# Engine programs without a block, loads released by matmul groups, larger evictions and an aligned TensorE loop in a batched matmul

## The chip, the cores and the metric

The kernel runs on one core of a Trainium2 chip. The metric is the device time of one execution in microseconds (us), as the median of several executions. A profiled execution also gives a span, from its first to its last instruction, which is about 2 us shorter than the time.

## The reference

```python
batch, m, k, n = 16, 512, 768, 1024      # x: [16, 768, 512], y: [16, 768, 1024], fp32
def reference(x, y):
    return np.einsum('bkm,bkn->bmn', x, y).astype(np.float32)
```

Each of the 16 batches loads 4.7 MB (x and y), multiplies, and stores 2.1 MB.

## The kernel before

SP (the SyncE engine) issues all transfers on one queue, VectorE casts x and y to bf16, TensorE multiplies in a loop of two batches per turn, and ScalarE copies PSUM to the output buffers. Input buffers are double, so the load of batch b reuses the buffers of batch b-2. Batches count from 0: the third load is that of batch 2, and where the prediction writes "load 3" it means batch 3. A release is the wait that lets SP issue a transfer, a landing is the semaphore count with which one of the 16 DMA engines reports the end of its part, and a hole is a time in which DMA engines have nothing to move. In the views PE is TensorE (PEld its weight loads), DVE VectorE, ACT ScalarE; a q marks the engine's sequencer, which waits and issues. `batch, i, first` of the TensorE program and the tensors are cut here.

```python
    @block.sync
    def _(sync):
        def store(b):
            sync.wait_ge(outs, b + 1)
            sync.dma_start(o_v[b], ob[b % NO][:]).then_inc(so[b % NO], 16)
        for b in range(B):
            i = b % 2
            if b >= 2:
                sync.wait_ge(cast, b - 1)            # both casts of batch b-2 are done
            sync.dma_start(xs[i][:], x_v[b]).then_inc(sx[i], 16)
            sync.dma_start(ys[i][:], y_v[b]).then_inc(sy[i], 16)
            if b >= LAG:                             # LAG = 4: the first store follows the fifth load
                store(b - LAG)
        # ... the last stores, the waits for all stores
    @block.vector
    def _(vector):
        for b in range(B):
            # ... wait for TensorE and for x; cast x, wait for y, cast y in two halves
            vector.drain().then_inc(cast, 1)
    @block.tensor
    def _(tensor):
        with tensor.Fori(0, B // 2):
            batch(tensor, 0, False)                  # 48 matmuls in 4 groups of 12
            batch(tensor, 1, False)
    @block.scalar
    def _(scalar):
        # ... one copy of 128x1024 for each group, then
            scalar.drain().then_inc(outs, 1)
```

## Time and profile before

| | before |
|---|---|
| time, median (first 3 runs) | 262.83 us |
| span | 261.2 us |
| DMA queue, share of 16 engines' span | 98.1% |
| moved | 109.05 MB |
| TensorE busy | 188.0 us |
| VectorE busy | 83.0 us |
| ScalarE busy | 66.1 us |

For the comparisons below, this is the view by stretches of time of the kernel before. The columns are the stretch, its length, five engines' busy time with instruction counts, TensorE's granted clock, DMA share and GB/s. DMA share is the second last.

```profile
24.00:28.00 4.00, 4.00 (x20) 2.09 (x19) 2.01 (x2) 1.42 (x2) 0.00 (x0) 1.00 0.97 415
...
34.00:36.00 2.00, 2.00 (x11) 1.02 (x9) 0.00 (x0) 0.64 (x1) 0.00 (x0) 1.00 0.85 363
36.00:40.00 4.00, 4.00 (x20) 2.13 (x19) 3.01 (x2) 1.39 (x2) 0.00 (x0) 1.00 1.05 440
...
48.00:52.00 4.00, 3.62 (x17) 1.51 (x15) 2.82 (x2) 2.03 (x2) 0.00 (x0) 1.00 1.03 436
52.00:56.00 4.00, 3.30 (x17) 1.74 (x17) 2.37 (x2) 1.01 (x1) 0.00 (x0) 1.00 1.10 449
```

The share lies between 0.85 and 1.10. It can pass 1, because a packet's whole time is counted in the stretch where it starts; a pause shows as a share clearly below that of the same stretch here.

### The profile page before, as it was taken

How to read it: one execution, taken by the hardware profiler on the slowest of the kernel's cores; microseconds unless marked ns; L12 is line 12 of the kernel's file. 1: busy time of each engine (PE TensorE's matmuls, PEld its weight loads, DVE VectorE, ACT ScalarE, POOL GpSimd, SP SyncE). 2: the span in 40 equal slices, each digit the busy share in tenths (PEclk: the TensorE clock that was granted, in tenths of full speed). 3: DMA queues.
4: the chain of work that ended last, by engine and by line, in shares of the span. 5: the costliest groups of instructions: out<-in, count | busy, mean ns of one | idle time of the engine just before them, and what ended most of it. 6: DMA issues, size and time to landing. Idle time of an engine off the chain costs nothing. (4 is left out here: it accounts for less than half of the span.)

```text
span 261.2 us, 1938 instructions
## 1 busy us (share of the span) xinstructions
PE 188.0 (72%) x768; PEld 87.1 (33%) x768; DVE 83.0 (32%) x48; ACT 66.1 (25%) x65; POOL 0.2 (0%) x4
## 2 busy tenths in 40 slices
PE   0039999998948949398595997939678394896920
PEld 0014555443513515144152342514334142342500
DVE  0261734435223252322524214252132523225000
ACT  1003343433331314114032140412314033131410
POOL 0000000000000000000000000000000000000000
PEclk9999999999986999979798697997999899797995
DMA  7999999999999999999999999999999999999993
GB/s 265 431 425 427 438 411 453 425 386 418 446 420 439 420 430 446 415 441 420 439 437 412 447 423 440 415 432 442 423 434 420 435 433 423 440 433 421 434 421 141
DMA packets 6915, 109.09 MB, mean 418 GB/s; under 512 B 768, under 2 KB 768, under 8 KB 768
## 3 DMA queue, kind: packets, MB, share of 16 engines
q1 hardware_dynamic: 6912, 109.05, 98.1%
q8 instruction: 1, 0.02, 0.0%
q14 instruction: 2, 0.02, 0.0%
HBM read 75.50 MB, written 33.55 MB: 417 GB/s over the span
## 5 line engine op out<-in xcount | busy, mean ns | idle before, releaser
L105 PE MATMUL ps<-yb,xb 128*128 128x512 bf16 x768 | 188.0, 406 | 61.6 <-PEq L100 55.9
L105 PEld LDWEIGHTS ps<-yb,xb 128*128 128x128 bf16 x768 | 87.1, 116 | 162.1 <-issue 96.7
L125 ACT COPY ob<-ps 128x1024 f32<-128x1024 f32 x64 | 64.9, 1013 | 183.6 <-PE ps L105 183.6
L93 DVE CAST yb<-ys 128x3072 bf16<-128x3072 f32 x32 | 54.9, 1757 | 88.4 <-DMA ys<-in_y_dram 88.4
L89 DVE CAST xb<-xs 128x3072 bf16<-128x3072 f32 x16 | 28.2, 1760 | 67.5 <-DMA xs<-in_x_dram 66.8
L125 ACT ACT_TABLE_LOAD x1 | 1.3, 1283 | 1.0 <-SPq L44 1.0
L142 POOL MEMSET const-uint8-127<- 128x1 uint8 x1 | 0.1, 102 | 0.0
L142 POOL MEMSET const-bfloat16-1.0<- 128x1 bf16 x1 | 0.1, 101 | 0.0
L142 POOL MEMSET const-float32-0.0<- 128x1 f32 x1 | 0.1, 98 | 0.2 <-issue 0.2
L142 POOL MEMSET const-float32-1.0<- 128x1 f32 x1 | 0.1, 98 | 0.0
## 6 DMA issues: line engine op xcount, KB each, us to landing
ys<-in_y_dram SPq DMA_DIRECT2D x16, 3072.0 KB, 27.7
out_dram<-ob SPq DMA_DIRECT2D x16, 2048.0 KB, 32.1
xs<-in_x_dram SPq DMA_DIRECT2D x16, 1536.0 KB, 20.8
```

The source lines that it names most:

```text
L89: nc.vector.tensor_copy(xb[i][:], xs[i][:]).then_inc(ready, 1)
L93: nc.vector.tensor_copy(yb[i][:, ks], ys[i][:, ks]).then_inc(ready, 1)
L105: mm = nc.tensor.matmul(ps[mo][:, nt], x_w[:, kt, mo], yb[i][:, kt, nt * NF:(nt + 1) * NF], start=(kt == 0), stop=(kt == KT - 1))
L125: nc.scalar.copy(ob[b % NO][:, mo].rearrange("p (t f) -> p t f", f=NF), ps[mo][:]).then_inc(room, 1)
L142: nc = _bacc.Bacc("TRN2", target_bir_lowering=False, num_devices=1)
```

## The change

The intent is fewer instructions. The block goes, and with it branches and a barrier; VectorE's 16 drains go; ScalarE makes 32 copies of 128x2048 instead of 64 of 128x1024; and the TensorE loop is put at the start of an instruction fetch block. With the drains, the semaphore `cast` is gone as well, so SP now releases loads and most stores by TensorE's group counter. Cut to its core:

```diff
-    ps = [ec(nc.psum_tensor(f"ps{i}", [P, NT, NF], FP32)) for i in range(MT)]
+    HB = MT // 2
+    ps = [ec(nc.psum_tensor(f"ps{i}", [P, HB, NT, NF], FP32)) for i in range(2)]
-    block = ec(nc.Block())
     # stores
-            sync.wait_ge(outs, b + 1)
+        if b < B - 2:
+            nc.sync.wait_ge(groups, 2 * (b + 2))
+        else:
+            nc.sync.wait_ge(outs, b - (B - 3))
     # loads
-                sync.wait_ge(cast, b - 1)
+            nc.sync.wait_ge(groups, 2 * (b - 2) + 1)     # TensorE's first half of batch b-2
     # VectorE
-            vector.drain().then_inc(cast, 1)
     # TensorE: two groups of 24 matmuls a batch
-        with tensor.Fori(0, B // 2):
+    with nc.Fori(0, B // 2, engines=OrderedEngineSet([pe]), head_slot={pe: 0}):
     # ScalarE: one copy of 128x2048 a group; a drain only in batch B - 2
     # ... cut
```

More of the change, by code (lines that the diff above doesn't have):

```diff
@@ L10 @@
 from concourse._compat import with_exitstack
+from concourse.ordered_engine_set import OrderedEngineSet
 @with_exitstack
@@ L41 @@
     KH = KT // 2
-    GP = NT * NF
     ctx.enter_context(tc.tile_critical())
@@ L54 @@
     so = [ec(nc.semaphore(f"so{i}")) for i in range(NO)]
-    cast = ec(nc.semaphore("cast"))
     ready = ec(nc.semaphore("ready"))
@@ L59 @@
     outs = ec(nc.semaphore("outs"))
-    block = ec(nc.Block())
-    @block.sync
-    def _(sync):
-        def store(b):
-            sync.wait_ge(outs, b + 1)
-            sync.dma_start(o_v[b], ob[b % NO][:]).then_inc(so[b % NO], 16)
-        for b in range(B):
-            i = b % 2
-            if b >= 2:
-                sync.wait_ge(cast, b - 1)
-            sync.dma_start(xs[i][:], x_v[b]).then_inc(sx[i], 16)
-            sync.dma_start(ys[i][:], y_v[b]).then_inc(sy[i], 16)
-            if b >= LAG:
-                store(b - LAG)
-        for b in range(B - LAG, B):
-            store(b)
-        for i in range(NO):
-            sync.wait_ge(so[i], 16 * len(range(i, B, NO)))
@@ L81, in _ @@
-    @block.vector
-    def _(vector):
-        for b in range(B):
-            i = b % 2
-            n = 16 * (b // 2 + 1)
-            if b >= 2:
-                vector.wait_ge(groups, MT * (b - 1))
-            vector.wait_ge(sx[i], n)
-            nc.vector.tensor_copy(xb[i][:], xs[i][:]).then_inc(ready, 1)
-            vector.wait_ge(sy[i], n)
-            for h in range(2):
-                ks = slice(h * KH, (h + 1) * KH)
-                nc.vector.tensor_copy(yb[i][:, ks], ys[i][:, ks]).then_inc(ready, 1)
-            vector.drain().then_inc(cast, 1)
@@ L96, in batch @@
-    def batch(tensor, i, first):
-        x_w = xb[i][:].rearrange("p k (j mo) -> p k mo j", mo=MT)
-        tensor.wait_ge(ready, 2).then_inc(ready, -2)
-        for mo in range(MT):
-            tensor.wait_ge(room, 1).then_inc(room, -1)
-            for nt in range(NT):
-                for kt in range(KT):
-                    if mo == 0 and nt == 0 and kt == KH:
-                        tensor.wait_ge(ready, 1).then_inc(ready, -1)
-                    mm = nc.tensor.matmul(
-                        ps[mo][:, nt], x_w[:, kt, mo],
-                        yb[i][:, kt, nt * NF:(nt + 1) * NF],
-                        start=(kt == 0), stop=(kt == KT - 1))
-            mm.then_inc(groups, 1)
@@ L111, in _, with store @@
-    @block.tensor
-    def _(tensor):
-        with tensor.Fori(0, B // 2):
-            batch(tensor, 0, False)
-            batch(tensor, 1, False)
-    @block.scalar
-    def _(scalar):
-        nc.scalar.nop().then_inc(room, MT)
-        for b in range(B):
-            for mo in range(MT):
-                if mo == 0 and b >= NO:
-                    scalar.wait_ge(so[b % NO], 16 * (b // NO))
-                scalar.wait_ge(groups, MT * b + mo + 1)
-                nc.scalar.copy(ob[b % NO][:, mo].rearrange("p (t f) -> p t f", f=NF),
-                               ps[mo][:]).then_inc(room, 1)
-            scalar.drain().then_inc(outs, 1)
+    def store(b):
+        if b < B - 2:
+            nc.sync.wait_ge(groups, 2 * (b + 2))
+        else:
+            nc.sync.wait_ge(outs, b - (B - 3))
+        nc.sync.dma_start(o_v[b], ob[b % NO][:]).then_inc(so[b % NO], 16)
@@ new lines @@
+    for b in range(B):
+        i = b % 2
+        if b >= 2:
+            nc.sync.wait_ge(groups, 2 * (b - 2) + 1)
+        nc.sync.dma_start(xs[i][:], x_v[b]).then_inc(sx[i], 16)
+        nc.sync.dma_start(ys[i][:], y_v[b]).then_inc(sy[i], 16)
+        if b >= LAG:
+            store(b - LAG)
+    for b in range(B - LAG, B):
+        store(b)
+    for b in range(B):
+        i = b % 2
+        n = 16 * (b // 2 + 1)
+        if b >= 2:
+            nc.vector.wait_ge(groups, 2 * (b - 1))
+        nc.vector.wait_ge(sx[i], n)
+        nc.vector.tensor_copy(xb[i][:], xs[i][:]).then_inc(ready, 1)
+        nc.vector.wait_ge(sy[i], n)
+        for h in range(2):
+            ks = slice(h * KH, (h + 1) * KH)
+            nc.vector.tensor_copy(yb[i][:, ks], ys[i][:, ks]).then_inc(ready, 1)
@@ new lines, in batch @@
+    def batch(i):
+        x_w = xb[i][:].rearrange("p k (j mo) -> p k mo j", mo=MT)
+        nc.tensor.wait_ge(ready, 2).then_inc(ready, -2)
+        for g in range(2):
+            nc.tensor.wait_ge(room, 1).then_inc(room, -1)
+            for m in range(HB):
+                for nt in range(NT):
+                    for kt in range(KT):
+                        if g == 0 and m == 0 and nt == 0 and kt == KH:
+                            nc.tensor.wait_ge(ready, 1).then_inc(ready, -1)
+                        mm = nc.tensor.matmul(
+                            ps[g][:, m, nt], x_w[:, kt, g * HB + m],
+                            yb[i][:, kt, nt * NF:(nt + 1) * NF],
+                            start=(kt == 0), stop=(kt == KT - 1))
+            mm.then_inc(groups, 1)
@@ new lines @@
+    pe = nc.tensor.engine
+    with nc.Fori(0, B // 2, engines=OrderedEngineSet([pe]), head_slot={pe: 0}):
+        batch(0)
+        batch(1)
+    nc.scalar.nop().then_inc(room, 2)
+    for b in range(B):
+        if b >= NO:
+            nc.scalar.wait_ge(so[b % NO], 16 * (b // NO))
+        for g in range(2):
+            nc.scalar.wait_ge(groups, 2 * b + g + 1)
+            cp = nc.scalar.copy(ob[b % NO][:, g * HB:(g + 1) * HB].rearrange("p m (t f) -> p m t f", f=NF),
+                                ps[g][:])
+            if b < B - 1:
+                cp.then_inc(room, 1)
+        if b == B - 2:
+            nc.scalar.drain().then_inc(outs, 1)
@@ L131 @@
+    cp.then_inc(outs, 1)
+    for i in range(NO):
+        nc.sync.wait_ge(so[i], 16 * len(range(i, B, NO)))
 _INS = ['x', 'y']
```

## The prediction

> **What bounds the kernel now.** I began with the page. Its busy shares put no compute engine over 72%, while the slice row for DMA reads 9 (90% or more) in every slice but the first and the last.
>
> ```profile
> PE 188.0 (72%) x768; PEld 87.1 (33%) x768; DVE 83.0 (32%) x48; ACT 66.1 (25%) x65; POOL 0.2 (0%) x4
> DMA  7999999999999999999999999999999999999993
> ...
> q1 hardware_dynamic: 6912, 109.05, 98.1%
> q8 instruction: 1, 0.02, 0.0%
> q14 instruction: 2, 0.02, 0.0%
> ```
>
> So the 16 DMA engines are the bound: 109.05 MB on one queue, 98.1% of 16 engines' span. In the trace's packet records a 16,384-byte packet takes 611 ns, so 16 engines move 16 x 16,384 / 611 = 429 GB/s, and 109.05 MB cannot take less than 254.2 us. The span is 261.2 us. Only the other 7 us can change: the start before the first packet, holes in the queue, engines that finish late, and the end.
>
> Next I read the waits of the DMA-issuing engine (SP), to see who decides when a transfer is queued (us in total, times, longest).
>
> ```profile
> SPq L72 <- DVEq L94: 188.5, 14, 15.5
> SPq L66 <- ACTq L127: 41.2, 4, 16.0
> SPq _compat.py:109 <- DMA out_dram<-ob: 4.8, 1, 4.8
> ```
>
> Loads wait for VectorE's drain after the casts. The last store waits for ScalarE, and then SP sits 4.8 us (to 259.80) until that store has landed.
>
> Then the timeline around the third load, because the change alters exactly what releases it.
>
> ```profile
> 18.49 0.33 SPq L72 DMA_DIRECT2D xs<-in_x_dram  x1
> ...
> 25.00 1.01 ACT L125 COPY ob<-ps 128x1024 f32<-128x1024 f32 x1 [1.57 <-PE ps L105]
> 25.99 3.43 DVE L93 CAST yb<-ys 128x3072 bf16<-128x3072 f32 x2 [5.55 <-DMA ys<-in_y_dram]
> ```
>
> The third load (batch 2) is issued at 18.49. The second ScalarE copy at 25.00 marks the end of TensorE's first 24 matmuls of batch 0. The cast at 25.99 marks that the second y tile has landed. The order of 18.5, 25.0 and 26.0 is the heart of this case.
>
> Last, the end in stretches of 1 or 2 us (the last two columns are DMA share and GB/s).
>
> ```profile
> 251.00:252.00 1.00, 0.00 (x0) 0.00 (x0) 0.00 (x0) 0.00 (x0) 0.00 (x0) 1.00 0.77 328
> ...
> 256.00:257.00 1.00, 0.00 (x0) 0.00 (x0) 0.00 (x0) 0.00 (x0) 0.00 (x0) 0.50 0.54 229
> 257.00:258.00 1.00, 0.00 (x0) 0.00 (x0) 0.00 (x0) 0.00 (x0) 0.00 (x0) 0.50 0.08 33
> 258.00:259.00 1.00, 0.00 (x0) 0.00 (x0) 0.00 (x0) 0.00 (x0) 0.00 (x0) 0.50 0.12 49
> 259.00:260.00 1.00, 0.00 (x0) 0.00 (x0) 0.00 (x0) 0.00 (x0) 0.00 (x0) 0.50 0.00 0
> ```
>
> One engine of 16 is a share of 0.0625. From 257 to 259 only one or two engines still work: laggards set the end, not the sum of bytes. In the semaphore records of the last store the median engine lands at 257.17, the second-latest at 259.05 and the latest at 259.79. I traced that spread back load by load. Until 36 us the latest engine is 0.77 behind the median. In the load that lands at 39.9 another engine is suddenly 1.98 behind, and it stays last (2.61 at the end). The only 16 KB "instruction" packet on q8 starts at 38.01 and takes 1,068 ns. So one instruction fetch seems to cost the latest engine over a microsecond, and with it the kernel.
>
> **What the Trainium skill says.** "DMA: Bandwidth & Descriptors", section Bandwidth, gives 435.2 GB/s as the fabric's ceiling over 16 ports; the trace agrees, with 429 from the packet and 418 mean. "Runtime: NRT & Kernel Launch", section Instruction fetch mechanics, says that sequencers refill instruction memory in 16 KiB blocks over their own DMA queue, and that a branch to a block that isn't resident forces such a fetch. The three instruction packets agree in kind, and q8's one in size; q14's two are 8 KB each. "ScalarE: Activation LUTs", section What ACT_TABLE_LOAD costs, has 0.833 ns per element plus a fixed 186 ns: 1,039 ns for 1,024 elements, where the trace has 1,013. "TensorE: Matmul & The Clock Gate", Part 1, says that the first microseconds after idleness run at half clock. Here the first 12 matmuls take about 5.2 us (17.05 to 22.3) and the next 12 take 2.59.
>
> **The change, part by part.**
> 1. No block. SP's entry branch goes, and so does one of the two barriers at the end. In the records SP passes the last wait at 259.80, starts the block's barrier at 259.96 and leaves it at 260.18. Removing it saves about 0.3 us; the entry, from 0.82 to 0.94, about 0.05. Both lie on the path. Sum: -0.35.
> 2. Loads released by TensorE's first half of batch b-2, not by the casts. In steady state this is 5 to 6.5 us later (in batch 13 the casts end at 223.2 and the second copy starts at 229.7). The queue can afford that: x takes 20.8 us from issue to landing, and its own data takes 8 packets of 460 ns = 3.7, so about 17 us are queued ahead of it. The first one cannot. Batch 2's load is issued at 25.0 instead of 18.5; first packets follow an issue by 0.8 to 1.0 us (0.94 to 1.95 at the start, 250.78 to 251.61 at the end), so at 25.9. The engines run out of load 1 between 24.4 and 25.6 (landings from 24.81 to 25.97, less 0.37 from last data to semaphore). This is a hole of about 1.1 us for the median engine but only 0.3 for the latest, whose lag it swallows. The following loads: load 3 would be issued near 35.4, with data queued to 37.1; load 4 near 45.7, with data to 48.3; from load 5 on a store lies between. No second hole, by margins of 1 to 2 us. Cost at the end: between +0.3 (the present second-latest engine) and +1.1 (a median one). I take +0.6.
> 3. TensorE's loop on a fetch boundary. Its body is 192 matmuls and weight loads plus a few waits, fewer than 256 instructions. Before, it probably straddled a block edge and the fetch came at 38 us, near the first branch back (36.6). Aligned, the fetch should be gone or come at the start, where the hole at 25 us would absorb its lag. Then the second-latest engine sets the end: 259.79 - 259.05 = -0.7. I give this 60%, so about -0.45.
> 4. 32 copies of 128x2048 for 64 of 128x1024: ScalarE 66 to about 61 us, all beside DMA. Only the last copy is on a path: 1,013 + 1,024 x 0.833 = 1.87 us, +0.85. The last store would be issued at 251.6 rather than 250.78. Its laggard takes that store up only at 253.85, and the second-latest likewise waits on its own earlier work, so this is hidden. Cost 0 to 0.2.
> 5. VectorE's 16 drains and SP's waits on them: off the path, 0. Later stores: also 0, since those of batches 12 to 14 are still issued several us before the queue reaches them.
>
> Sum: -0.35 + 0.6 - 0.45 + 0.1 = -0.1. The parts are small and of both signs, and I shade slightly to the gain, since the hole may also swallow other engines' early lag: 262.6 us.
>
> **The rivals.** First, the hole wins: the fetch still comes after 25 us, on one engine, and the median's whole 1.1 us is lost. Then 262.8 - 0.35 + 1.1 = about 263.6. For it: the timeline's 25.0 plus 0.9 lies after the median end of load 1. Against: none of the fetch's cause is proved. Second, the fetch was everything: lag gone and hole at its minimum, 262.8 - 0.35 + 0.3 - 0.7 = about 262.0, or 261.5 if TensorE warms up earlier and no hole opens. Third, TensorE's wait takes the place of the cast as a new bound in every batch, because a load now depends on the matmuls that depend on the load before it: a hole of 1 us in each of 14 batches would make 275. Against it stand the 17 us of queue and the margins above; the margin is thinnest in batches 3 and 4. Fourth, the doubled last copy is exposed: +0.85, 263.4; the late laggards speak against it.
>
> **Range and chances.** Rivals one and two span 262.0 to 263.6; the clock's warm-up can move the hole by another half microsecond. So 261.5 to 263.8 should hold 8 times in 10. Two per cent is 5.3 us. The DMA floor of 254.2 plus start and end leaves no such gain; a loss needs the third rival.
>
> **What would show it.** The same 109.05 MB at about 98%. SP's load waits now on TensorE. The third load issued near 25.0, and a drop of DMA share between 24.5 and 26 that isn't repeated at 36 or 47 us. No q8 packet near 38 us, and fewer laggards in the last 2 us. One barrier less after the last landing. Last copy about 1.87 us. I am wrong if DMA share drops in each batch, if the q8 fetch stays and the same lag with it, or if the last store's late issue delays the last landing.

## The result

| | before | changed |
|---|---|---|
| time, median of 6 runs | 263.04 us | 265.34 us |
| lowest to highest | 262.77 to 263.68 | 264.81 to 266.19 |
| span of the profiled run | 261.2 us | 262.9 us |
| ratio, 95% interval | | 1.0087 (1.0065 to 1.0109) |

The changed kernel is 0.9% slower, clear of noise though within 2%. The predicted 262.6 and its range of 261.5 to 263.8 both miss it. From the page of the changed kernel:

```profile
PE 192.6 (73%) x768; PEld 87.5 (33%) x768; DVE 83.0 (32%) x48; ACT 61.1 (23%) x33; POOL 0.2 (0%) x4
...
DMA  7997999999999999999999999999999999999995
GB/s 266 443 423 307 400 396 430 408 426 400 446 414 436 438 414 447 416 443 418 424 451 414 447 416 439 436 418 439 424 432 441 417 447 418 440 424 429 426 414 229
...
q1 hardware_dynamic: 6912, 109.05, 97.8%
q8 instruction: 1, 0.02, 0.0%
q14 instruction: 1, 0.01, 0.0%
```

The same bytes move, and ScalarE has the predicted 61 us. In the row of DMA digits there is one new 7, in the fourth slice (19.7 to 26.3 us), where the rate falls to 307 GB/s. The timeline of SP, ScalarE and VectorE in that region shows what was issued when:

```profile
25.39 0.33 SPq L78 DMA_DIRECT2D xs<-in_x_dram  x1
25.39 1.87 ACT L127 COPY ob<-ps 128x2048 f32<-128x2048 f32 x1 [23.14 <-PE ps L109]
25.76 0.43 SPq L79 DMA_DIRECT2D ys<-in_y_dram  x1
26.91 3.43 DVE L96 CAST yb<-ys 128x3072 bf16<-128x3072 f32 x2 [5.52 <-DMA ys<-in_y_dram]
```

The third load is issued at 25.39 instead of 18.49, in the same instant as ScalarE's first copy, because both wait for TensorE's first 24 matmuls. The stretches of the changed kernel beside those of before:

```profile
24.00:28.00 4.00, 4.00 (x20) 2.05 (x19) 1.08 (x1) 1.87 (x1) 0.00 (x0) 1.00 0.47 154
...
34.00:36.00 2.00, 2.00 (x11) 1.03 (x10) 0.00 (x0) 0.25 (x1) 0.00 (x0) 1.00 1.00 430
36.00:40.00 4.00, 4.00 (x20) 2.14 (x19) 1.17 (x1) 1.62 (x1) 0.00 (x0) 1.00 0.95 363
...
48.00:52.00 4.00, 4.00 (x20) 2.04 (x18) 1.07 (x1) 1.02 (x1) 0.00 (x0) 1.00 0.98 399
```

From 24 to 28 the DMA share is 0.47 where it was 0.97: 4 x 0.50 = 2.0 us of all 16 engines' time are lost there. At 34 to 40 and at 48 to 52, where the next two loads begin, no hole is seen (0.95 to 1.00, and 0.98). The waits of SP answer to those shown of before (us in total, times, longest):

```profile
SPq L78 <- PE ps L109: 196.7, 14, 22.4
...
SPq L44 <- DMA out_dram<-ob: 4.8, 1, 4.8
...
SPq L71 <- ACTq L132: 1.6, 1, 1.6
```

All 14 load waits now end with TensorE. And the end:

```profile
258.00:259.00 1.00, 0.00 (x0) 0.00 (x0) 0.00 (x0) 0.00 (x0) 0.00 (x0) 0.50 1.19 508
259.00:260.00 1.00, 0.00 (x0) 0.00 (x0) 0.00 (x0) 0.00 (x0) 0.00 (x0) 0.50 0.69 295
260.00:261.00 1.00, 0.00 (x0) 0.00 (x0) 0.00 (x0) 0.00 (x0) 0.00 (x0) 0.50 0.19 82
261.00:262.00 1.00, 0.00 (x0) 0.00 (x0) 0.00 (x0) 0.00 (x0) 0.00 (x0) 0.50 0.00 0
```

Most engines are still at work at 259, where in the kernel before only laggards were left. From the semaphore records of the two profiled runs (each transfer adds 16 single counts, one from each DMA engine):

| landing | before | changed | later by |
|---|---|---|---|
| y of batch 1, median engine | 25.20 | 25.14 | -0.06 |
| x of batch 2, median | 28.90 | 31.17 | 2.27 |
| x of batch 3, median | 39.88 | 42.39 | 2.51 |
| x of batch 5, median | 67.24 | 70.10 | 2.86 |
| x of batch 15, median | 225.61 | 228.37 | 2.76 |
| last store, median | 257.17 | 260.32 | 3.15 |
| last store, latest engine | 259.79 | 261.68 | 1.89 |
| end of the span | 261.23 | 262.89 | 1.66 |

So most is lost in one place, between 24 and 31 us, and 0.6 us more by batch 5. From then to batch 15 the loads of the two kernels run in step, 2.8 to 2.9 us apart. At the end part of it is returned: the latest engine is 1.36 us behind the median instead of 2.61, and one barrier less takes 0.23 us off (1.21 instead of 1.44 from last landing to end). The median is later here than at batch 15 because the engines that are on time now wait for the last store to be issued (254.14 instead of 250.78). The latest engine doesn't: its last store lands 4.84 us after the one before, as before the change (4.83).

The packet records of the trace show a second thing. They mark a few packets as instruction fetches. The one of 16 KB, on q8, came at 38.01 before, and comes at 3.99 now. In the first load one DMA engine is now 1.77 us behind the median (0.75 before), so x and y of batch 0 land about 1 us later (the first cast of y starts at 15.95 instead of 14.99), and TensorE starts at 18.01 instead of 17.05. That the fetch makes this engine late is inferred from its timing: in all 13 profiled runs the transfer in progress at that fetch, early or late, has an engine 1.7 to 2.2 us behind.

### The profile page after: what moved, and what is told of

It is laid out like the page before. It is cut to its first block, busy times and chain, and to the rows that moved or that the text cites. A ratio compares the mean times of both kernels' runs of the same rounds, so it can differ in the third digit from the quotient of the medians.

```text
span 262.9 us, 1831 instructions
## 1 busy us (share of the span) xinstructions
PE 192.6 (73%) x768; PEld 87.5 (33%) x768; DVE 83.0 (32%) x48; ACT 61.1 (23%) x33; POOL 0.2 (0%) x4
## 5 line engine op out<-in xcount | busy, mean ns | idle before, releaser
L109 PE MATMUL ps<-yb,xb 128*128 128x512 bf16 x768 | 192.6, 413 | 59.6 <-PEq L103 53.3
L127 ACT COPY ob<-ps 128x2048 f32<-128x2048 f32 x32 | 59.8, 1868 | 192.1 <-PE ps L109 192.1
```

The lines of the kernel that those rows point to most:

```text
L109: mm = nc.tensor.matmul(ps[g][:, m, nt], x_w[:, kt, g * HB + m], yb[i][:, kt, nt * NF:(nt + 1) * NF], start=(kt == 0), stop=(kt == KT - 1))
L127: cp = nc.scalar.copy(ob[b % NO][:, g * HB:(g + 1) * HB].rearrange("p m (t f) -> p m t f", f=NF), ps[g][:])
```

## The experiments

My theory after the result was: the loss is the late release of the third load, one hole in the DMA queue. Rivals were a cost in every batch because loads now depend on TensorE, the earlier instruction fetch, and the doubled last copy.

**1. The third load alone is released by the casts.**

```diff
+            if b == 2:
+                nc.sync.wait_ge(cast, 1)
+            else:
                 nc.sync.wait_ge(groups, 2 * (b - 2) + 1)
+        if b == 0:
+            nc.vector.drain().then_inc(cast, 1)
```

> The changed kernel, but the third load (batch 2) alone is released by VectorE's casts again; all other loads still wait for TensorE's first half. My theory: the loss is one hole in the DMA queue at that load (median landing of load 2's x 2.27 us later than before). Then the load is issued near 19.5 instead of 25.39, there is no hole near 25, the landings of batch 3 to 15 lie within 0.6 us of the kernel before, and the time falls from 265.3 to 262.0 to 263.3 (level with before or up to 1 us better). Rival (a wait on TensorE in every batch, a shallower queue): the time stays above 264.5, because 13 of the 14 waits are unchanged. Rival (doubled last copy or the early instruction fetch): also no more than 0.5 us better.

Measured: 265.45 us beside 262.95 of before, ratio 1.0093 (1.0077 to 1.0110). The expected 262.0 to 263.3 was missed. It gained nothing, and my theory of a single guilty wait fell. The stretches show why:

```profile
24.00:28.00 4.00, 4.00 (x21) 2.08 (x19) 0.99 (x1) 1.87 (x1) 0.00 (x0) 1.00 0.92 390
...
34.00:36.00 2.00, 2.00 (x11) 1.07 (x10) 0.00 (x0) 0.00 (x0) 0.00 (x0) 1.00 0.58 246
36.00:40.00 4.00, 4.00 (x20) 2.10 (x19) 2.03 (x2) 1.87 (x1) 0.00 (x0) 1.00 0.71 233
```

The hole at 24 is gone, and the same hole stands at 35: against before, 2 x (0.85 - 0.58) + 4 x (1.05 - 0.71) = 1.9 us. The third load being on time, the data queued for it end at 35.75 (landing 36.12 less 0.37); the fourth load waits for TensorE's half of batch 1 and is issued at 36.15, with first packets at 37.10. In the changed kernel the hole at the third load had hidden that the fourth was late as well.

**2. All loads released by the casts.**

```diff
-            nc.sync.wait_ge(groups, 2 * (b - 2) + 1)
+            nc.sync.wait_ge(cast, b - 1)
     # after VectorE's last cast of each batch
+        nc.vector.drain().then_inc(cast, 1)
```

> The changed kernel with all 14 loads released by the casts, through a drain as before. My theory: the same time as with batch 2 alone so released (within 0.4 us), since the other 13 releases had queue to spare. Rival (each batch loses a little): clearly better than with batch 2 alone, by 0.5 us or more. Either way the engine that fetches TensorE's instructions at 4 us keeps its lag of about 1.8 us, now that no hole swallows it.

Measured: 262.88 us beside 262.95, ratio 0.9996 (0.9983 to 1.0009). That is 2.6 us better than experiment 1, so the expectation (level with it) was missed. The whole loss comes from the release of the loads. What remains of the change (no block, aligned loop, larger copies, later stores) is worth nothing that can be told from noise. One thing is worth knowing: the last store was issued at 253.32 instead of 250.78, in part by the longer copy, and the median engine landed it at 259.50, only 0.35 us before the latest one. The late engine just hides it.

**3. The kernel before with the late release.**

```diff
-                sync.wait_ge(cast, b - 1)
+                sync.wait_ge(groups, MT * (b - 2) + MT // 2)
```

> The kernel before with one line changed: loads wait for half of TensorE's matmuls of batch b-2 instead of the casts. Block, small copies and unaligned loop stay. My theory: the third load is issued near 25.0, first packets at 25.9, a hole of 1.1 us for the median engine plus 0.4 or more for slow packets after the restart, so 1.5 to 2.3 us slower than before: 264.5 to 265.3; the fetch at 38 us stays, after the hole, so its lag of about 1.6 us stays at the end. Rival (the change's other parts are to blame): within 0.5 us of before.

Measured: 266.34 us beside 262.95, ratio 1.0124 (1.0105 to 1.0143). This one line is enough for the loss and more. It is about 1 us above what I expected. In this run there is a second hole, from 48 to 52:

```profile
24.00:28.00 4.00, 4.00 (x21) 2.08 (x19) 2.58 (x2) 2.03 (x2) 0.00 (x0) 1.00 0.67 237
...
48.00:52.00 4.00, 4.00 (x20) 2.13 (x19) 1.75 (x2) 1.78 (x2) 0.00 (x0) 1.00 0.83 298
```

The fetch stays at 37.4, just when y of batch 2 lands (1.95 us later on one engine than on the median). By this timing TensorE gets batch 2 late and with it the release of the fifth load, issued at 47.74: its first packet comes at 48.70, and the median engine's data ahead of it had ended at 48.28.

**4. The changed kernel without the loop's alignment.**

```diff
-    with nc.Fori(0, B // 2, engines=OrderedEngineSet([pe]), head_slot={pe: 0}):
+    with nc.Fori(0, B // 2, engines=OrderedEngineSet([pe])):
```

> The changed kernel without the loop's place on a fetch boundary. My theory: the 16 KB fetch moves from 4 us back to some 38 us, the first y tile lands about 1 us earlier, TensorE's first half ends 0.4 to 1 us earlier, and the hole gets that much shorter; but the fetch's lag now comes after the hole and stays to the end. Sum between -0.6 and +0.8 us against the changed kernel, so 264.7 to 266.1. Rival (the early fetch is the whole loss): 263.0 or less.

Measured: 266.92 us beside 262.95, ratio 1.0140 (1.0124 to 1.0156), slower than I expected and slower than the changed kernel (1.0087). The fetch is back, at 38.11, and the third load is issued earlier, at 24.87, as expected. But again a second hole opens:

```profile
24.00:28.00 4.00, 4.00 (x20) 2.13 (x19) 2.54 (x2) 1.87 (x1) 0.00 (x0) 1.00 0.64 215
...
48.00:52.00 4.00, 4.00 (x20) 2.11 (x19) 1.02 (x1) 1.87 (x1) 0.00 (x0) 1.00 0.78 280
```

The first hole is smaller than in the changed kernel (0.64 against 0.47) and the second one is new (0.78 against 0.98 in the changed kernel and 1.03 before). The early fetch is therefore not what slows the changed kernel. With this late release the aligned loop with its early fetch helps, by some 1.4 us by the two ratios (0.53% of 263); with the early release the kernel that has both is level with before (experiment 2).

**5 and 6. How late is too late: the kernel before, released by the first and by the third of four groups.**

```diff
-                sync.wait_ge(cast, b - 1)
+                sync.wait_ge(groups, MT * (b - 2) + 1)     # and + 3 in the other
```

> The kernel before, loads released by the first of TensorE's four groups of batch b-2 instead of the casts. My theory now: only the release relative to the end of the data queued ahead counts. The first group ends near 22.4, first packets at 23.3, before load 1's data end (24.8), so no hole there; load 3 near 32.7 to 33, also in time (35.8). So level with before, within 0.8 us (262.2 to 263.7). Rival (any dependence of loads on TensorE costs something in each batch): 264 or more.

Measured: 263.02 us beside 263.09, ratio 0.9995 (0.9981 to 1.0009). Loads depend on TensorE in every batch here and nothing is lost, so the dependence as such costs nothing. The third load was issued at 21.95.

> The same with the third group. My theory: released 2.6 us later than with half (266.3), so the hole at the third load grows by some 2.6 us to about 5, and since TensorE, at 10.4 us a batch against 11.0 us of data, hardly catches up, later loads 3 to 5 lose too: 269 to 273. Rival (the loss is a fixed cost of the dependence, not a matter of lateness): like half, 266 to 267.

Measured: 273.29 us beside 263.09, ratio 1.0398 (1.0363 to 1.0434), 0.3 us above what I expected. There are two large holes:

```profile
24.00:28.00 4.00, 4.00 (x20) 2.13 (x19) 2.31 (x2) 1.78 (x2) 0.00 (x0) 1.00 0.28 74
...
48.00:52.00 4.00, 4.00 (x20) 2.06 (x19) 0.00 (x0) 2.03 (x2) 0.00 (x0) 1.00 0.59 252
52.00:56.00 4.00, 4.00 (x20) 2.14 (x19) 3.30 (x2) 1.02 (x1) 0.00 (x0) 1.00 0.35 89
```

Against before these lose 4 x 0.69 = 2.8 us and 4 x (0.44 + 0.75) = 4.8 us. So the three releases, 2.6 us apart on TensorE, cost 0, 3.4 and 10.2 us. Beyond the point where the release is in time, the cost grows faster than the lateness, since several loads miss.

**7. The changed kernel with four groups and small copies.** The release points in TensorE's work stay where they are.

```diff
-    HB = MT // 2
-    ps = [ec(nc.psum_tensor(f"ps{i}", [P, HB, NT, NF], FP32)) for i in range(2)]
+    HB = MT // 4
+    ps = [ec(nc.psum_tensor(f"ps{i}", [P, HB, NT, NF], FP32)) for i in range(4)]
-            nc.sync.wait_ge(groups, 2 * (b - 2) + 1)
+            nc.sync.wait_ge(groups, 4 * (b - 2) + 2)
     # ... all other counts of groups doubled, four copies a batch
```

> The changed kernel with four groups of 12 matmuls and 64 copies of 128x1024 again; releases at the same points in TensorE's work as in the changed kernel. My theory: the last copy shrinks from 1.87 to 1.01 us and the last store is issued 0.85 us earlier, but the latest DMA engine takes that store up later than its issue, so the time stays within 0.4 us of the changed kernel (264.9 to 265.8). Rival (the doubled last copy is part of the loss): 0.85 us better, 264.5 or less.

Measured: 265.92 us beside 263.09, ratio 1.0108 (1.0091 to 1.0125): no gain, and 0.1 us above what I expected. The last copy is short again:

```profile
253.68 1.01 ACT L127 COPY ob<-ps 128x1024 f32<-128x1024 f32 x1 [1.57 <-PE ps L109]
```

The doubled last copy is no part of the loss. The median is 0.6 us above the changed kernel's, but the intervals of the two ratios overlap. A difference would agree with the fetch, at which one engine fell 2.2 us behind here instead of 1.8, so the third load was issued at 26.11; with one profile of each this isn't shown.

**8. All loads released by the casts, the loop at slot 48 of a fetch block.**

```diff
-    with nc.Fori(0, B // 2, engines=OrderedEngineSet([pe]), head_slot={pe: 0}):
+    with nc.Fori(0, B // 2, engines=OrderedEngineSet([pe]), head_slot={pe: 48}):
```

> The changed kernel with all loads released by the casts (262.9), and the loop placed at slot 48 of a fetch block rather than slot 0. If the 16 KB fetch on q8 comes from the loop lying in another block than the code ahead of it, and that code is shorter than 48 slots, the fetch is gone, no engine is 1.7 us late, y of batch 15 lands up to 2 us earlier and the time falls to 260.5 to 262. If the fetch stays (near 4 or 38 us), the time stays at 262.5 to 263.2.

Measured: 263.09 us beside 263.09, ratio 0.9996 (0.9983 to 1.0009). The fetch stays, at 4.23 us. What sets it off remains open. In all 13 profiled runs it came near 4 us with a loop placed by slot and at 37 to 38 us without.

**9. The loads of batches 2, 3 and 4 released by the casts, the other 11 by TensorE.** This is the test of the theory that took the place of the first: TensorE is late only while the queue holds loads alone.

```diff
+            if b <= 4:
+                nc.sync.wait_ge(cast, b - 1)
+            else:
                 nc.sync.wait_ge(groups, 2 * (b - 2) + 1)
+        if b <= 2:
+            nc.vector.drain().then_inc(cast, 1)
```

> The changed kernel, with the loads of batches 2, 3 and 4 released by the casts and the other 11 still by TensorE. My corrected theory: TensorE is late only while the queue holds loads alone, that is until the first stores; by the numbers its release misses the data queued ahead by 1.6, 0.95 and 0.3 us at the third, fourth and fifth load, and from the sixth on there is slack. Then this is level with all loads released by the casts: 262.5 to 263.3, no hole anywhere. Rival (every TensorE wait costs): still 264.5 or more.

Measured: 262.76 us beside 263.06, ratio 0.9995 (0.9981 to 1.0008). Releasing these three loads early removes the whole loss; that the first alone is not enough was seen in experiment 1, the first two alone weren't tried. The stretches have no hole left:

```profile
24.00:28.00 4.00, 4.00 (x21) 2.09 (x19) 0.97 (x1) 1.87 (x1) 0.00 (x0) 1.00 0.96 409
...
34.00:36.00 2.00, 2.00 (x11) 1.08 (x10) 0.00 (x0) 0.51 (x1) 0.00 (x0) 1.00 0.91 387
36.00:40.00 4.00, 4.00 (x20) 2.09 (x19) 1.99 (x2) 1.36 (x1) 0.00 (x0) 1.00 1.05 445
```

**10. Which engine is late.** Sixteen tiny transfers behind the last load, on the base of experiment 2. The Trainium skill, "DMA: Bandwidth & Descriptors", section Why a DMA increments its semaphore by 16 and not by 1, says that a transfer of k rows from SP runs on the lowest-numbered k engines.

```diff
+        if b == B - 1:
+            for k in range(16):
+                nc.sync.dma_start(pr[0:k + 1, k], x_v[0][0:k + 1, 0, 0:32]).then_inc(sk[k], 16)
     # ... and waits for the 16 semaphores at the end
```

> All loads released by the casts, and behind the last load 16 tiny transfers of 1, 2, ... 16 rows, each on its own semaphore. By the skill's account a transfer of k rows runs on the k lowest-numbered DMA engines, so the first transfer that lands some 2 to 3 us later than the one before it shows which of the 16 engines is the latest. No theory of the change hangs on it; the time should stay within 1 us of 262.9. It is to tell whether that engine could be relieved: only the highest-numbered one can be left out of a transfer by the count of rows.

Measured: one look, 263.98 us, state unknown, so its time is not compared. The records agree with the page in the count: after one early count at the issue, the transfer of k rows shows k landings. The one of 10 rows was complete at 234.63 and the one of 11 rows at 235.71, where y of batch 15 also ended (235.54). That step is 1.1 us, not the expected 2 to 3, but it is the largest, and it reaches the end of the load. If the numbering is as the page has it, the late engine is the eleventh of 16. It cannot be left out by the number of rows without leaving out the five above it, so I did not try to relieve it.

**11. A mended version.** It is the kernel of experiment 7, released one group earlier.

```diff
-            nc.sync.wait_ge(groups, 4 * (b - 2) + 2)
+            nc.sync.wait_ge(groups, 4 * (b - 2) + 1)
```

> The changed kernel with four groups, its loads released by the first group of batch b-2 (one group earlier than in the run with four groups). By my theory this mends the change without VectorE's drains: release near 23.5, first packets near 24.5, just before the median end of load 1 (24.8), so no hole to speak of. One barrier less than before should give -0.3, the early fetch's lag stays on one engine as in the kernel with all loads released by the casts. So 262.4 to 263.2, level with before or a few tenths better; three us better than with the second group (265.9).

Measured: 263.00 us beside 263.02, ratio 0.9989 (0.9974 to 1.0004). One group earlier is worth 2.9 us. A small hole remains, against the expectation:

```profile
24.00:28.00 4.00, 4.00 (x20) 2.11 (x19) 0.78 (x1) 1.87 (x2) 0.00 (x0) 1.00 0.78 289
```

Against before that is 4 x 0.19 = 0.8 us. In the profiled run the median engine lands the last store 1.29 us later than before; a smaller lag of the latest engine (1.83 instead of 2.61) and the barrier (0.23) leave 0.3 us of it in the span. The six runs (262.08 to 263.39) are level with the kernel before and don't beat it clearly. No kernel in this study does.

## Why the prediction was wrong

**What held.** The DMA queue bounds both kernels. The barrier was worth 0.23 us (predicted about 0.3, with 0.35 for the block in all); removing the block gave nothing at the start, since SP's first transfer is issued at 0.94 in both. The last copy took 1.87 us, as predicted, and it was hidden behind the late engines, as experiment 7 confirms. The fetch moved to the start and the hole then swallowed its lag: no engine was more than 0.34 us behind the median in the next load. The release at 25 us did open a hole that the median engine felt. No second hole followed in the changed kernel: by the issues at 35.75 and 47.14 plus 0.96 us, and the end of the data ahead at 38.10 and 49.32, the next two loads kept margins of 1.4 and 1.2 us.

**The step that failed is part 2 of the sum: "Cost at the end: between +0.3 (the present second-latest engine) and +1.1 (a median one). I take +0.6."** The mechanism was right and the size was not: the last landing came 1.89 us later, and the hole measured 2.0 us of DMA time and 2.27 in the median landing, where 1.1 was expected. Three terms were missing.

First, I took 25.0 for the release from the kernel before, but y of batch 0 landed later, at the early fetch. TensorE began about 1 us later, and though its first 24 matmuls took 7.4 us instead of 8.0, its first half ended only at 25.39. The first packet came at 26.36 instead of the 25.9 worked out, 1.6 us after the median engine's data had ended (24.77). Nor do all engines start together: by a count of the packet records, which don't name the engine, nine take their first packet between 26.36 and 26.64 and seven only from 27.03 to 27.13. Over the 16 engines the standing still comes to 1.95 us each.

Second, the restart isn't free. In the packet records of the changed kernel 17 packets of 12,288 bytes that start between 26.3 and 27.4 take 0.09 to 0.88 us longer than the usual 460 ns. Their excess adds up to 7.0 us, or 0.44 us for each of 16 engines. The next two loads start slowly too, although no hole stands before them: their x packets have 6.1 and 2.4 us of excess, 0.53 us an engine. Standing still and slow starts together, 1.95 + 0.44 + 0.53 = 2.9 us, account for the 2.8 to 2.9 us that the kernels are apart from batch 5 to batch 15. What such starts have in common is a late issue. Over the loads of batches 2 to 4 in 12 of the profiled runs (all but experiment 10), the excess of a load's x packets was 7.0 to 10.9 us where the first packet followed the issue by 0.96 us, 1.2 to 7.2 at 1.8 to 2.2 us, 1.5 and 1.1 at 2.6 and 2.9 us, and at most 0.5 from 3.2 us on. Why is open, and no run tests it alone. So a margin of 1 to 2 us avoids a hole but not a slow start.

Third, I let the second-latest engine of before set the end after losing only 0.3 in the hole. But this hole lasted until the latest engine had run out too (26.52), and it levelled the engines (1.75 us behind before it, 0.33 after), so that engine's earlier lag says nothing of the end. Lag then grew again, to 1.22 us at the slow start of batch 3's load and 1.80 at batch 4's, and was 1.36 us at the last store. This is less than the 2.61 of before but on top of a median that is 3.15 later: 3.15 + 1.36 - 2.61 = 1.9, and less the barrier's 0.23, 1.7 in the span.

**The margins for later loads** were worked out only behind the first hole, and there they held. Experiment 1 shows what they hide. In the opening there are loads alone in the queue, and each takes 11.0 us (x of batch 2 to x of batch 3 in the kernel before: 28.90 to 39.88). TensorE takes 10.36 us a batch (copies at 25.39 and 35.75). Having started late, it gains only 0.6 us per batch on the data: it misses by 1.6, 0.95 and 0.3 us at the third, fourth and fifth load (an estimate from these numbers). A hole at one of them shifts the data and so excuses the next. Then the first stores stand between the loads and give slack: in the changed kernel the sixth load is issued 6.2 us before its first packet. Experiment 9 shows no loss at any load after these three.

**The third rival**, TensorE as the new bound in every batch, was rejected on good grounds for the steady state: experiments 5 and 9 show that. **Rivals one and two** bracketed the hole by 0.3 and 1.1; the range built on them was too narrow because both took the release time from the kernel before and neither had slow starts. The "275" of the third rival is a slip: 262.8 - 0.35 + 14 is 276.5. In part 4, 253.85 is where the second-latest engine takes up the last store; the latest does at 254.55, which makes the margin larger. The 256 instructions of part 3 are the size of a 16 KiB block in the section Instruction fetch mechanics that the prediction cites; that the loop had straddled one stays unproved.

## What to carry to other kernels

When a buffer's release is moved from its last reader to a later event, compare that event with the end of the data queued ahead at every load of the opening, where the queue is shallow, not with the steady state's depth; and do it with each earlier load on time, since one hole hides the next. A wait that is harmless by 2 us cost 3.4 when it came 2.6 us later. Don't stop at "no hole": here the loads issued less than some 3 us before their first packet began with slow packets. A fix that removes one late wait and changes nothing has not cleared the mechanism: look whether the hole has moved.

## What the Trainium skill lacked or had wrong

- "Runtime: NRT & Kernel Launch", section Instruction fetch mechanics, speaks of 16 KiB blocks; here the instruction packets on q14 are of 8 KB (309 to 333 ns inside the kernel, 578 ns for one at the end of experiment 10), and only the one on q8 has 16 KB. The section calls the cost of crossing a block mostly hidden and says nothing of the data traffic; here, at the q8 fetch (922 to 1,322 ns), one DMA engine falls 1.7 to 2.2 us behind the median, and in the five fast runs without a hole the latest engine is still 2.1 to 2.8 us behind at the last store but one.
- No page that I read says that a load issued shortly before its data can flow starts slowly: 17 packets with 0.44 us of excess per engine after the hole, slow starts of the next two loads without one (0.38 and 0.15 us), and the first 16 packets of the kernel before take 962 to 1,744 ns instead of 460.
- "ScalarE: Activation LUTs", section What ACT_TABLE_LOAD costs, gives 186 ns plus 0.833 ns per element for an ACTIVATE with immediate scale and bias, and no figure of its own for a copy; the copies here take 1,013 ns for 1,024 and 1,868 ns for 2,048 elements, about 25 ns less than estimates by that formula (1,039 and 1,892 ns).
